# A recurrent layer's block inverse packed into half the columns, and its key and output blocks run with wide matmuls

## The chip, the cores and the metric

The kernel runs on one core of a Trainium2 chip. The metric is the time of one execution on the device, in microseconds (us). TensorE does the matmuls, VectorE (DVE) and ScalarE (ACT) the elementwise work, GpSimd (POOL) small copies; SyncE (SP) issues the DMAs. Each engine works through its instructions in a fixed order.

## What is computed

The reference is a trunk of two layers over 256 tokens with 2048 channels: a differential attention with a gated convolution MLP, then a gated DeltaNet layer with another such MLP. The change is in the DeltaNet layer. Cut to that layer:

```python
qkv = silu(causal_dwconv(qkv, conv_w))          # of h @ w_in
q, k = l2_norm(q), l2_norm(k)                   # 16 heads, repeated to 32
low = where(strict, (k_beta @ k.T) * decay, 0)  # per head and chunk of 64 tokens
a_mat = low + eye(64)                           # unit lower triangular
u = triangular_solve(a_mat, v_beta)
w = triangular_solve(a_mat, k_beta * exp(g_c))
# then a scan over the chunks with state, q, k, u, w
o = rms_norm(o, norm_g) * silu(z)
x = x + o @ w_out
```

## The kernel before

**Two-part matmuls.** Every weight tile comes from DRAM in 512 KB pieces (`raw`, L86), called tiles below. ScalarE casts a piece to a short float type (`whi`, L89), and VectorE subtracts to get the rest (`wlo`, L90). Four buffers of each kind rotate. Activations are held in two parts as well, 256 columns each. The function `dense` multiplies such a piece: 4 row blocks by 2 column tiles. *Wide* means one matmul of `whi` with both activation parts (512 columns, L151) and one of `wlo` with the first part (256 columns, L152), into two halves of a PSUM bank that are added afterwards. *Narrow* means three matmuls of 256 columns (L151, L152, L154) into one half, so there is nothing to add.

**The DeltaNet stage** (`gdn`) goes through 4 batches of 4 key heads. Per batch it runs 4 key blocks (`k`), a value block (`v`), two gate blocks (`z`, in `dense_tok`), 3 more value blocks, and then the 8 output blocks of the batch before. A key or value block is 16 row blocks long, so 4 tiles of 8 steps; an output block has 8 row blocks and 2 tiles. A small gate projection of 4 tiles runs ahead of the first batch. Key blocks and the last batch's value blocks are narrow, the other value blocks wide; an output block is narrow in batches 0 to 2 for its first four column blocks.

Beside this stream, coroutines do the rest, and each advances when `dense` calls `tick()` after a tile: `keys` (squares, sums, exponentials of the decay rows `lt` that come back from DRAM through `grow`, products, copies of the diagonal blocks into `cc` by GpSimd), `invert` (the inverse of all 32x32 diagonal blocks of a batch), `levels` (joins the 32s to 64s and 128s), `group` (solves and output). A scheduler then sets each engine's order by its own timeline.

**The inverse.** Each of the four groups of 32 partitions holds 16 blocks of 32x32 per batch. `cc` has 32 columns, of which 16 are filled; VectorE transposes it so that partition = block, and 16 of every 32 partitions work on zeros. A loop over 30 columns j then multiplies and subtracts on `Ti` (L667, L670), with `(31-j) * j` elements each time. Two transposes give `ttc` and `tcc`. The tiles share the tag `s4` with three buffers.

**The edges of the stage.** The constants `con` (identity and mask) are loaded at its start, into memory that the layer before used until its end.

Of the kernel before, what the change touches and what calls it, by code (L numbers as in the profile page):

```python
# [16 lines left out]
P = 128  # L17
T = 256
D = 2048
KD = D // P  # L20
# [6 lines left out]
class Trunk:  # L27
# [514 lines left out]
    def gdn(self, w_gate, w_in, w_z, w_out, nb, hb, gate_ap, const_ap, conv_col, ng, done):  # L542
# [7 lines left out]
        nc, tc, mp = self.nc, self.tc, self.mp  # L550
        nq = nb * hb
# [3 lines left out]
        with tc.tile_pool(name="gd", bufs=1) as gd:  # L555
# [3 lines left out]
            ident, mask = con[:, :P], con[:, P:]  # L559
# [9 lines left out]
                nc.gpsimd.memset(Tas[i][:64], 0.0)  # L569
            quad = [slice(32 * s, 32 * s + 32) for s in range(4)]  # L570
            flat = "p i c -> p (i c)"
            gates, lows = {}, []

            def lin(w, wide):
# [19 lines left out]
            def keys(hq, c, cc, b0, res):  # L594

                sq = gd.tile([P, 2, T], F32, tag="qs", name="qs", bufs=2)
                nc.scalar.square(sq, c)
                sp = gd.tile([P, 2, 2, T], F32R, tag="qp", name="qp", bufs=1)
                lows.append(self.split(sp, sq))

                def fetch():
                    d = gd.tile([P, 2, 384], F32, tag="lt", name="lt", bufs=hb)
                    nc.sync.dma_start(d, gates["rows"][2 * hq:2 * hq + 2, :].unsqueeze(0).to_broadcast([P, 2, 384]))
                    return d

                d = fetch() if "rows" in gates else None
                yield
                yield
                while "rows" not in gates:
                    yield  # L610
                if d is None:
                    d = fetch()
                    yield
                    yield
                    yield
                gc = gates["col"]
                dv = d[:, :, :T].rearrange("p v (t c) -> p v t c", t=2)
                m4 = mask.unsqueeze(1).unsqueeze(1).to_broadcast([P, 2, 2, P])
                pn = mp()
                sums = self.total(pn, [sp])  # L620
                while len(lows) < 2:
                    yield
                with tc.issue_after(lows[max(hq, 1)].ins):
                    nc.vector.tensor_tensor(dv, dv, m4, ALU.add)
                with self.lnexp(sums):
                    self.rsqrt(sq, self.apart(pn), 1)
                    for v in range(2):
                        for t, s in ((1, d[:, v, :P]), (0, d[:, v, P:])):
                            nc.scalar.activation(s, s, AF.Exp, bias=gc[:, t, 2 * hq + v:2 * hq + v + 1])
                nc.vector.tensor_tensor(c, c, sq, ALU.mult)  # L630
                q, k = c[:, 0, :], c[:, 1, :]
                yield
                yield
                prods = []
                for r in (k, q):
                    p = mp()
                    nc.tensor.matmul(p[:, :P], k[:, P:], r[:, P:], start=True, stop=True)
                    nc.tensor.matmul(p[:, P:384], k[:, :P], r, start=True, stop=True)  # L638
                    prods.append(p)
                lt = d  # L640
                qkt = gd.tile([P, 2, 384], F32, tag="qkt", name="qkt", bufs=hb)
                for v in range(2):
                    nc.vector.scalar_tensor_tensor(
                        qkt[:, v], prods[1][:, :384], P ** -0.5, d[:, v], ALU.mult, ALU.mult)
                    nc.vector.tensor_tensor(lt[:, v], prods[0][:, :384], d[:, v], ALU.mult)
                for v in range(2):
                    b = b0 + v
                    lv = lt[:, v, :T].rearrange("p (t c) -> p t c", t=2)
                    for r in quad:
                        nc.gpsimd.tensor_copy(  # L650
                            cc[r, :, 2 * b:2 * b + 2].rearrange("p c t -> p t c"), lv[r, :, r])
                    res.append((lt[:, v], qkt[:, v]))

            def invert(cc, lqs, inv):

                while len(lqs) < 2 * hb:
                    yield
                x = gd.tile([P, 32, 32], F32, tag="s4", name="X", bufs=3)
                nc.vector.transpose(x.rearrange(flat), cc.rearrange(flat))
                t = gd.tile([P, 32, 32], F32, tag="s4", name="Ti", bufs=3)  # L660
                nc.vector.tensor_scalar(t, x, -1.0, None, ALU.mult)
                nc.vector.memset(t.rearrange(flat)[:, ::33], 1.0)
                for j in range(1, 31):
                    m = 31 - j
                    tmp = gd.tile([P, T], F32, tag="tmp", name="tmp", bufs=1)
                    w = tmp[:, :m * j].rearrange("p (i c) -> p i c", c=j)
                    nc.vector.tensor_tensor(  # L667
                        w, x[:, j + 1:, j:j + 1].to_broadcast([P, m, j]),
                        t[:, j:j + 1, :j].to_broadcast([P, m, j]), ALU.mult)
                    nc.vector.tensor_tensor(t[:, j + 1:, :j], t[:, j + 1:, :j], w, ALU.subtract)  # L670
                    if j % 3:
                        yield
                ttc = gd.tile([P, 32, 32], F32, tag="s4", name="ttc", bufs=3)
                nc.vector.transpose(ttc.rearrange("p m i -> p i m"), t)
                tcc = gd.tile([P, 32, 32], F32, tag="s4", name="tcc", bufs=3)
                nc.vector.transpose(tcc.rearrange("p m c -> p c m"), t.rearrange("p i c -> p c i"))
                inv += [ttc, tcc]

            def levels(lqs, inv, gs, done):
# [137 lines left out]

            def out(b, acts):
                for blk in range(KD // 2):
                    wide = b == nb - 1 or blk >= KD // 4  # L820
                    ps = self.dense(w_out[b * (KD // 2) + blk], 2 * hb, lambda k: self.await_(acts, k), wide=wide)
                    self.add_out(blk, ps, done if b == nb - 1 else None, wide)

# [2 lines left out]
            pend = None  # L826
            for b in range(nb):
                heads = range(b * hb, (b + 1) * hb)
                cc = gd.tile([P, 32, 32], F32, tag="s4", name="Cc", bufs=3)
                nc.gpsimd.memset(cc, 0.0)  # L830
                lqs, inv, solved, acts, zts = [], [], [], [], {}
                groups = [range(i, i + gh) for i in range(0, hb, gh)]
                plan = [("k", i) for i in range(hb)] + [("v", 0)] + [("z", g) for g in range(len(groups))]
                for op, i in plan + [("v", i) for i in range(1, hb)]:
                    if op == "k":
                        hq = heads[i]
                        c = convs(lin(w_in[hq * 2], False), (hq, nq + hq))
                        self.spawn(keys(hq, c, cc, 2 * i, lqs))
                        if i == hb - 1:
                            self.spawn(invert(cc, lqs, inv))  # L840
                            self.spawn(levels(lqs, inv, range(len(groups)), solved))
                    elif op == "z":
                        gr = groups[i]
                        zt = zts[i] = gd.tile([P, 2, gv, P], F32, tag="vz", name="zt", bufs=4)
                        ps = self.dense_tok(w_z[heads[gr[0]] // 2], KD, self.h_acts)
                        for t in range(2):
                            nc.scalar.activation(zt[:, t].rearrange(flat), ps[:, t, :], AF.Silu,  # L847
                                                 scale=self.rstdc[:, t:t + 1])
                    else:
                        gi = i // gh  # L850
                        gr = groups[gi]
                        if i == gr[0]:
# [223 lines left out]
```

## Time and profile before

| | |
|---|---|
| median of 3 runs | 2532.01 us (2531.71 to 2532.07) |
| the profiled execution | 2531.32 us, span 2529.5 us |
| instructions | 42709 |
| granted TensorE clock | 1.00 throughout |
| DMA | 487.25 MB, mean 193 GB/s |
| DeltaNet stage | from 1053.9 us (first matmul of its gate block) to 1848.9 us |

Times in rows are us from the span's start. A row of the order of time has start, duration, engine, line, operation, tiles written and read, matrix size, shape and count; in brackets stands how long the engine was idle before, and what ended that. A row of a group ends with count, busy time, mean ns of one, idle time before. Matmuls overlap in the records: what one costs in a stream is the distance between starts, not its duration.

### The profile page before, as it was taken

Reading aid. Unit: us, or ns where it says so; the run is one execution under the profiler, and the core shown is the slowest. Engines: PE = TensorE matmul, PEld = TensorE weight load, DVE = VectorE, ACT = ScalarE, POOL = GpSimd, SP = SyncE. Lnnn points to the kernel's source line nnn. Section 1 sums busy time; section 2 is a strip of 40 time slices with the busy share of each in tenths; the row PEclk is TensorE's granted clock in tenths of the full one; section 3 lists DMA queues with packets and bytes.
Section 4 is the critical chain, followed back from the end, with each engine's and each line's share of the span. In section 5 each row is a group of like instructions: output and inputs, shape, how many; then the busy total and the mean of one; then the engine's idle time right before and its main releaser. Section 6 shows DMA issues by size and latency. Waiting matters only on the chain.

```text
span 2529.5 us, 42709 instructions
## 1 busy us (share of the span) xinstructions
PE 2522.4 (100%) x16727; PEld 2330.5 (92%) x16727; DVE 1913.4 (76%) x2822; ACT 1501.8 (59%) x2082; POOL 97.2 (4%) x189
## 2 busy tenths in 40 slices
PE   9999999999999999999999999999999999999999
PEld 8998899999999999999989989999999999999998
DVE  8886677777777555689879789788787777776544
ACT  7766656666666444485674675674566666665343
POOL 0000000000000000011110021021000000000000
PEclk9999999999999999999999999999999999999999
DMA  7555566666666666666555555555466666666665
GB/s 257 175 183 175 167 204 201 201 201 201 201 201 202 201 199 201 203 189 207 163 170 197 162 183 190 163 186 174 162 201 200 202 201 201 201 202 205 210 207 157
DMA packets 138203, 487.25 MB, mean 193 GB/s; under 512 B 15473, under 2 KB 18449, under 8 KB 138001
## 3 DMA queue, kind: packets, MB, share of 16 engines
q1 hardware_dynamic: 137712, 484.17, 60.0%
q8 instruction: 131, 2.15, 0.4%
q14 instruction: 72, 0.58, 0.1%
q10 hardware_dynamic: 288, 0.35, 0.0%
HBM read 482.32 MB, written 2.15 MB: 192 GB/s over the span
## 4 chain that ended last, share of the span: by engine, by line
PE 99%; DMA 1%; DVE 0%; ACT 0%; SPq 0%; issue 0%; ACTq 0%
PE ps L151 50%; PE ps L152 27%; PE ps L154 4%; PE ps L221 3%; PE ps L220 3%; PE ps L222 3%; PE mp L765 2%; PE mp L151 1%; PE mp L329 1%; PE mp L638 1%; PE mp L152 0%; PE ps L123 0%; PE mp L730 0%; PE mp L748 0%; PE mp L810 0%; PE mp L466 0%
## 5 line engine op out<-in xcount | busy, mean ns | idle before, releaser
L90 DVE TENSOR_TENSOR wlo<-raw,whi 128x1024 fp32r<-128x1024 f32 (+2 forms) x911 | 1102.6, 1212 | 510.2 <-ACT whi L89 502.0
L89 ACT CAST whi<-raw 128x1024 fp32r<-128x1024 f32 (+2 forms) x911 | 944.1, 1038 | 849.9 <-PE ps L151 627.1
L151 PE MATMUL ps<-h,whi 128*128 128x512 f32 (+1 forms) x4208 | 1348.0, 366 | 0.0
L152 PE MATMUL ps<-h,wlo 128*128 128x256 f32 x4208 | 1151.2, 274 | 0.6 <-DVE wlo L90 0.6
L151 PEld LDWEIGHTS ps<-h,whi 128*128 128x128 f32 x4208 | 797.2, 189 | 93.6 <-ACT zt L847 0.2
L152 PEld LDWEIGHTS ps<-h,wlo 128*128 128x128 f32 x4208 | 807.7, 192 | 2.0 <-DVE wlo L90 0.9
L151 PE MATMUL ps<-ac,whi 128*128 128x512 f32 x1546 | 506.8, 382 | 0.0
L152 PE MATMUL ps<-ac,wlo 128*128 128x256 f32 x1546 | 421.2, 273 | 0.0
L151 PEld LDWEIGHTS ps<-ac,whi 128*128 128x128 f32 x1546 | 292.1, 189 | 40.6 <-PE ps L151 0.2
L152 PEld LDWEIGHTS ps<-ac,wlo 128*128 128x128 f32 x1546 | 296.8, 192 | 0.1
L154 PE MATMUL ps<-h,whi 128*128 128x256 f32 x656 | 181.8, 277 | 0.0
L151 PE MATMUL ps<-oc,whi 128*128 128x512 f32 (+1 forms) x512 | 159.7, 344 | 0.0
L220 PE MATMUL ps<-whi,h 128*128 128x512 f32 x384 | 146.4, 381 | 0.0
L221 PE MATMUL ps<-wlo,h 128*128 128x512 f32 x384 | 145.8, 380 | 0.0
L222 PE MATMUL ps<-whi,h 128*128 128x512 f32 x384 | 145.8, 380 | 0.0
L310 DVE SCALAR_TENSOR_TENSOR cv<-u,fcols,cv 128x255 f32<-128x255 f32 (+1 forms) x344 | 142.9, 477 | 0.0
L152 PE MATMUL ps<-oc,wlo 128*128 128x256 f32 x512 | 140.7, 275 | 0.0
L154 PEld LDWEIGHTS ps<-h,whi 128*128 128x128 f32 x656 | 125.8, 192 | 0.2
L151 PEld LDWEIGHTS ps<-oc,whi 128*128 128x128 f32 x512 | 97.4, 190 | 8.0
L152 PEld LDWEIGHTS ps<-oc,wlo 128*128 128x128 f32 x512 | 98.3, 192 | 0.3
L308 ACT ACTIVATE cv<-u,fcols 128x256 f32<-128x256 f32 x172 | 93.9, 593 | 0.6 <-DVE u L205 0.5
L310 DVE SCALAR_TENSOR_TENSOR cv<-u,cols,cv 128x255 f32<-128x255 f32 (+2 forms) x192 | 84.2, 478 | 0.4 <-ACT cv L306 0.3
(222 smaller groups left out, 2178.7 us busy)
## 6 DMA issues: line engine op xcount, KB each, us to landing
raw<-w_up SPq DMA_DIRECT2D x344, 512.0 KB, 4.7
raw<-w_down SPq DMA_DIRECT2D x160, 512.0 KB, 3.7
raw<-w_in SPq DMA_DIRECT2D x128, 512.0 KB, 4.6
raw<-w_z SPq DMA_DIRECT2D x64, 512.0 KB, 3.8
raw<-w_out SPq DMA_DIRECT2D x64, 512.0 KB, 4.3
raw<-w_qk SPq DMA_DIRECT2D x56, 512.0 KB, 4.6
raw<-w_v SPq DMA_DIRECT2D x32, 512.0 KB, 3.5
raw<-w_o SPq DMA_DIRECT2D x32, 512.0 KB, 4.7
```

Source lines behind the costliest of these rows:

```text
L89: self.cast = nc.scalar.copy(hi[:, :, s], raw[:, :, s])
L90: nc.vector.tensor_tensor(lo[:, :, s], raw[:, :, s], hi[:, :, s].bitcast(F32), ALU.subtract)
L151: nc.tensor.matmul(bank[c][:, :n], hi[:, k, s], self.turns(a[:, :n // T, :]), start=first, stop=False)
L152: nc.tensor.matmul(bank[c][:, :T], lo[:, k, s], self.turns(a[:, :1, :]), start=False, stop=last and wide)
L154: nc.tensor.matmul(bank[c][:, :T], hi[:, k, s], self.turns(a[:, 1:, :]), start=False, stop=last)
L220: nc.tensor.matmul(ps[:, c, :], ah, wh, start=first, stop=False)
L221: nc.tensor.matmul(ps[:, c, :], ah, wl, start=False, stop=False)
L222: nc.tensor.matmul(ps[:, c, :], al, wh, start=False, stop=last)
L308: nc.scalar.activation(out, u, AF.Identity, bias=bias, scale=taps[n - 1])
L310: nc.vector.scalar_tensor_tensor(out[:, j:], u[:, :T - j], taps[n - 1 - j], out[:, j:], ALU.mult, ALU.add)
L329: last = self.nc.tensor.matmul(out, self.onesr, self.pairs(p[:, j]), start=i + j == 0, stop=i + j == n)
L765: nc.tensor.matmul(p[:, v, :], l(v), r[:, v, :], start=i == 0, stop=i == len(terms) - 1)
```

## The change

The inverse uses all 32 partitions of a group: `cc` has only the 16 filled columns, the transpose reads it twice (16 partitions each), and `Ti` holds the even columns of the inverse in one set of 16 partitions and the odd ones in the other, 16 columns wide. The loop has 31 steps with `(31-j) * (j//2 + 1)` elements. `Ti` is filled by GpSimd with zeros and with ones where the diagonal lies; which parity a partition has comes from `half`, which VectorE reduces once from `ident` (a part of `con`). `tcc` comes from `Ti`, and `ttc` from `tcc`. Each tile has a tag and one buffer of its own. `keys` yields three times instead of two. Key blocks of batches 0 to 2 and all output blocks are wide.

```diff
+            nl = 4 * hb
+            half = gd.tile([P, 2], F32, tag="half", name="half")
...
-                yield
-                yield
+                for _ in range(3):
+                    yield
...
-            def invert(cc, lqs, inv):
+            def invert(b, cc, lqs, inv):
+                while not lqs:
+                    yield
+                if b == 0:
+                    nc.vector.tensor_reduce(half, ident.rearrange("p (q a c) -> p a q c", q=4, a=2), AX.XY, ALU.add)
+                t = gd.tile([P, 32, 16], F32, tag="Ti", name="Ti")
+                nc.gpsimd.memset(t, 0.0)
+                for a in range(2):
+                    nc.gpsimd.tensor_copy(t.rearrange(flat)[:, 16 * a::33], half[:, a:a + 1].to_broadcast([P, 16]))
                 while len(lqs) < 2 * hb:
                     yield
-                x = gd.tile([P, 32, 32], F32, tag="s4", name="X", bufs=3)
-                nc.vector.transpose(x.rearrange(flat), cc.rearrange(flat))
-                t = gd.tile([P, 32, 32], F32, tag="s4", name="Ti", bufs=3)
-                nc.vector.tensor_scalar(t, x, -1.0, None, ALU.mult)
-                nc.vector.memset(t.rearrange(flat)[:, ::33], 1.0)
-                for j in range(1, 31):
-                    m = 31 - j
+                x = gd.tile([P, 32, 32], F32, tag="X", name="X")
+                nc.vector.transpose(x, cc.unsqueeze(2).to_broadcast([P, 32, 2, nl]))
+                for j in range(31):
+                    m, n = 31 - j, j // 2 + 1
...
-                    w = tmp[:, :m * j].rearrange("p (i c) -> p i c", c=j)
+                    w = tmp[:, :m * n].rearrange("p (i c) -> p i c", c=n)
...
-                    nc.vector.tensor_tensor(t[:, j + 1:, :j], t[:, j + 1:, :j], w, ALU.subtract)
+                    nc.vector.tensor_tensor(t[:, j + 1:, :n], t[:, j + 1:, :n], w, ALU.subtract)
...
-                nc.vector.transpose(ttc.rearrange("p m i -> p i m"), t)
-                nc.vector.transpose(tcc.rearrange("p m c -> p c m"), t.rearrange("p i c -> p c i"))
+                tcc = gd.tile([P, nl, 32], F32, tag="tcc", name="tcc")
+                nc.vector.transpose(tcc.rearrange("p m (c a) -> p c a m", a=2), t.rearrange("p i c -> p c i"))
+                ttc = gd.tile([P, nl, 32], F32, tag="ttc", name="ttc")
+                nc.vector.transpose(ttc.rearrange(flat), tcc.rearrange(flat))
...
-                    wide = b == nb - 1 or blk >= KD // 4
+                    wide = True
...
-                cc = gd.tile([P, 32, 32], F32, tag="s4", name="Cc", bufs=3)
-                nc.gpsimd.memset(cc, 0.0)
+                cc = gd.tile([P, 32, nl], F32, tag="Cc", name="Cc")
...
-                        c = convs(lin(w_in[hq * 2], False), (hq, nq + hq))
+                        c = convs(lin(w_in[hq * 2], b<nb-1), (hq, nq + hq))
```

In the new file later lines have moved: L629 became L631, L591 L593, L597 L599, L704 L711, the key block's narrow eviction L196 became a copy L582, an addition L583 and a scaling L205.

The scheduler's order moves with it. VectorE at the start of the stage, before (L343 adds the last block of the layer before into x; the 512-wide L90 is the gate block's last piece, the 1024-wide the first key block's):

```order
L90 TENSOR_TENSOR wlo<-raw,whi 128x512
L343 TENSOR_TENSOR x<-ps,x 128x512
L90 TENSOR_TENSOR wlo<-raw,whi 128x1024
L235 SCALAR_TENSOR_TENSOR h<-x,cols,h 128x256 x2
L247 TENSOR_TENSOR ss<-ss,sq 128x256
```

The same place now:

```order
L90 TENSOR_TENSOR wlo<-raw,whi 128x512
L343 TENSOR_TENSOR x<-ps,x 128x512
L661 TENSOR_REDUCE half<-con 128x2
L90 TENSOR_TENSOR wlo<-raw,whi 128x1024
L235 SCALAR_TENSOR_TENSOR h<-x,cols,h 128x256 x2
L247 TENSOR_TENSOR ss<-ss,sq 128x256
```

The reduction of `half` from `con` is put ahead of the first key block's piece.

ScalarE in batch 0, around the first exponentials of the decay rows (L629), before:

```order
L89 CAST whi<-raw 128x1024
L321 CAST qp<-qs 128x512
L591 ACT_TABLE_LOAD
L591 ACTIVATE cv<-cv 128x512
L89 CAST whi<-raw 128x1024
L597 ACTIVATE qs<-cv 128x512
L629 ACT_TABLE_LOAD
L629 ACTIVATE lt<-lt,gc 128x128
```

And now (L631):

```order
L89 CAST whi<-raw 128x1024
L321 CAST qp<-qs 128x512
L89 CAST whi<-raw 128x1024
L593 ACT_TABLE_LOAD
L593 ACTIVATE cv<-cv 128x512
L599 ACTIVATE qs<-cv 128x512
L89 CAST whi<-raw 128x1024
L582 COPY u<-ps 128x512
L631 ACT_TABLE_LOAD
L631 ACTIVATE lt<-lt,gc 128x128
```

Two casts stand between L321 and the exponentials instead of one, and the new copy L582 too.

TensorE where the joining of batch 0's inverse begins (L704, reading `tcc`), before, in the second key block of batch 1:

```order
L151 MATMUL ps<-h,whi 128x256
L704 MATMUL mp<-tcc,lt 32x32 x32
L748 MATMUL mp<-con,cv 128x128 x4
L152 MATMUL ps<-h,wlo 128x256
L154 MATMUL ps<-h,whi 128x256
```

And now (L711), in the last value block of batch 0:

```order
L151 MATMUL ps<-h,whi 128x512
L711 MATMUL mp<-tcc,lt 32x32 x32
L152 MATMUL ps<-h,wlo 128x256
L151 MATMUL ps<-h,whi 128x512
L152 MATMUL ps<-h,wlo 128x256
```

It has moved six tiles ahead in the stream of blocks.

More of the change, by code (lines that the diff above doesn't have):

```diff
@@ L665, in invert @@
+                nc.vector.transpose(x, cc.unsqueeze(2).to_broadcast([P, 32, 2, nl]))
+                for j in range(31):
+                    m, n = 31 - j, j // 2 + 1
                     tmp = gd.tile([P, T], F32, tag="tmp", name="tmp", bufs=1)
-                    w = tmp[:, :m * j].rearrange("p (i c) -> p i c", c=j)
+                    w = tmp[:, :m * n].rearrange("p (i c) -> p i c", c=n)
                     nc.vector.tensor_tensor(
-                        w, x[:, j + 1:, j:j + 1].to_broadcast([P, m, j]),
-                        t[:, j:j + 1, :j].to_broadcast([P, m, j]), ALU.mult)
@@ L670, in invert @@
-                    nc.vector.tensor_tensor(t[:, j + 1:, :j], t[:, j + 1:, :j], w, ALU.subtract)
+                        w, x[:, j + 1:, j:j + 1].to_broadcast([P, m, n]),
+                        t[:, j:j + 1, :n].to_broadcast([P, m, n]), ALU.mult)
+                    nc.vector.tensor_tensor(t[:, j + 1:, :n], t[:, j + 1:, :n], w, ALU.subtract)
                     if j % 3:
                         yield
-                ttc = gd.tile([P, 32, 32], F32, tag="s4", name="ttc", bufs=3)
-                nc.vector.transpose(ttc.rearrange("p m i -> p i m"), t)
@@ L675, in invert @@
-                tcc = gd.tile([P, 32, 32], F32, tag="s4", name="tcc", bufs=3)
-                nc.vector.transpose(tcc.rearrange("p m c -> p c m"), t.rearrange("p i c -> p c i"))
+                tcc = gd.tile([P, nl, 32], F32, tag="tcc", name="tcc")
+                nc.vector.transpose(tcc.rearrange("p m (c a) -> p c a m", a=2), t.rearrange("p i c -> p c i"))
+                ttc = gd.tile([P, nl, 32], F32, tag="ttc", name="ttc")
+                nc.vector.transpose(ttc.rearrange(flat), tcc.rearrange(flat))
@@ L836, in gdn @@
                         hq = heads[i]
-                        c = convs(lin(w_in[hq * 2], False), (hq, nq + hq))
+                        c = convs(lin(w_in[hq * 2], b<nb-1), (hq, nq + hq))
                         self.spawn(keys(hq, c, cc, 2 * i, lqs))
                         if i == hb - 1:
-                            self.spawn(invert(cc, lqs, inv))
+                            self.spawn(invert(b, cc, lqs, inv))
                             self.spawn(levels(lqs, inv, range(len(groups)), solved))
```

## The prediction

> **What bounds the kernel now.** I read the page's first parts, then who TensorE waited for, then stretches of the DeltaNet stage (1054 to 1849 us), where the change lies. First the page's busy times and, below them, the chain that ended last by engine:
>
> ```profile
> PE 2522.4 (100%) x16727; PEld 2330.5 (92%) x16727; DVE 1913.4 (76%) x2822; ACT 1501.8 (59%) x2082; POOL 97.2 (4%) x189
> PE 99%; DMA 1%; DVE 0%; ACT 0%; SPq 0%; issue 0%; ACTq 0%
> ```
>
> A busy TensorE can still be one that stutters, so the waits decide. This is the only wait of TensorE that the list of waits has after the first layer's start (0.6 us in total, once):
>
> ```profile
> PE ps L152 <- DVE wlo L90: 0.6, 1, 0.6
> ```
>
> So the kernel is TensorE's stream of matmuls. Time is won only by a shorter stream, and lost only where VectorE (DVE) or ScalarE (ACT) hands over a weight tile too late. Four stretches of the stage; the columns are TensorE, weight loads, VectorE, ScalarE and GpSimd busy, each with its count, then granted clock, DMA share and GB/s:
>
> ```profile
> 1053.90:1107.00 53.10, 53.10 (x466) 52.65 (x465) 44.10 (x80) 38.25 (x55) 3.92 (x6) 1.00 0.70 224
> 1165.00:1196.40 31.40, 31.40 (x193) 28.88 (x192) 30.75 (x59) 17.68 (x22) 0.00 (x0) 1.00 0.62 200
> 1350.40:1371.80 21.40, 21.40 (x194) 21.40 (x193) 21.26 (x39) 10.95 (x13) 0.00 (x0) 1.00 0.63 210
> 1394.50:1456.30 61.80, 61.80 (x668) 60.98 (x667) 43.51 (x74) 38.87 (x60) 1.69 (x3) 1.00 0.49 159
> ```
>
> The first and last are narrow key blocks (the first with the gate block ahead), the second wide value blocks beside the inverse, the third narrow output blocks beside the inverse. Beside the inverse VectorE is at 98 and 99%; in the key stretches at 83 and 70%. Weight loads fill 100% of the narrow output stretch and 92% of the wide one. The clock is 1.00 throughout.
>
> **The change part by part.**
>
> *Narrow blocks made wide.* A narrow block issues three 256-column matmuls per weight tile, a wide one a 512-column and a 256-column matmul: the same 768 columns, one weight load less. The changed blocks hold 12 x 16 x 2 = 384 key triples and 12 x 8 x 2 = 192 output triples, 576 in all. What a triple and a pair take is read from starts in the order of time. The 64 triples of the third stretch, from the first row to the last (the next block's first):
>
> ```profile
> 1350.36 0.28 PE L151 MATMUL ps<-oc,whi 128*128 128x256 f32 x1
> 1350.47 0.28 PE L152 MATMUL ps<-oc,wlo 128*128 128x256 f32 x1
> 1350.59 0.28 PE L154 MATMUL ps<-oc,whi 128*128 128x256 f32 x1
> ...
> 1371.80 0.38 PE L151 MATMUL ps<-oc,whi 128*128 128x512 f32 x1
> L154 PE MATMUL ps<-oc,whi 128*128 128x256 f32 x64 | 17.6, 275 | 0.0
> ```
>
> (1371.80 - 1350.36) / 64 = 0.3350 us. The 96 pairs of the second stretch:
>
> ```profile
> 1165.02 0.38 PE L151 MATMUL ps<-h,whi 128*128 128x512 f32 x1
> ...
> 1196.46 0.28 PE L151 MATMUL ps<-h,whi 128*128 128x256 f32 x1
> L151 PE MATMUL ps<-h,whi 128*128 128x512 f32 x96 | 31.5, 382 | 0.0
> ```
>
> (1196.46 - 1165.02) / 96 = 0.3275 us. A triple becomes a pair for 7.5 ns less: 576 x 7.5 = **4.3 us off TensorE's stream**. Reading error is 0.01 us at either end, so under 0.2 us in the sum. The Trainium skill, page "TensorE: Matmul & The Clock Gate", section "Back-to-back issue gap", gives an isolated gap of N / 2.4 + 2.5 ns: 327.5 ns for the triple and 325.0 for the pair, thus 1.4 us in the sum by it. The rows are of this very stream, so 4.3 is used.
>
> *What the wide form adds beside the stream.* A narrow key block leaves PSUM by one VectorE operation (the first row), a wide one by a ScalarE copy, an addition and a scaling; a wide output block adds into x twice instead of once:
>
> ```profile
> L196 DVE TENSOR_TENSOR u<-ps,rstd 128x512 f32<-128x512 f32 x20 | 13.7, 686 | 2.2 <-PE ps L154 2.1
> L580 ACT COPY u<-ps 128x512 f32<-128x512 f32 x12 | 6.9, 576 | 0.0
> L581 DVE TENSOR_TENSOR u<-ps,u 128x512 f32<-128x512 f32 x12 | 8.2, 682 | 0.0
> L205 DVE TENSOR_TENSOR u<-u,rstd 128x512 f32<-128x512 f32 x98 | 67.7, 691 | 2.9
> L343 DVE TENSOR_TENSOR x<-ps,x 128x512 f32<-128x512 f32 x98 | 67.3, 687 | 10.3 <-PE ps L152 6.9 <-PE ps L154 2.1
> ```
>
> Per key block 0.69 us on VectorE and 0.58 on ScalarE, per output block 0.69 on VectorE: 16.5 us of VectorE and 6.9 of ScalarE in all.
>
> *The inverse.* One batch's, between 1149 and 1212 us:
>
> ```profile
> L667 DVE TENSOR_TENSOR tmp<-X,Ti 128x30 f32<-128x30 f32 (+14 forms) x30 | 9.8, 327 | 0.6
> L670 DVE TENSOR_TENSOR Ti<-Ti,tmp 128x30 f32<-128x30 f32 (+14 forms) x30 | 9.8, 327 | 0.4
> L676 DVE STREAM_TRANSPOSE tcc<-Ti 128x1024 f32<-128x1024 f32 x1 | 2.1, 2095 | 0.0
> L674 DVE STREAM_TRANSPOSE ttc<-Ti 128x1024 f32<-128x1024 f32 x1 | 2.0, 2004 | 0.0
> L659 DVE STREAM_TRANSPOSE X<-Cc 128x1024 f32<-128x1024 f32 x1 | 1.2, 1248 | 0.9 <-POOL Cc L650 0.9
> L667 DVE TENSOR_TENSOR tmp<-X,Ti 128x30 f32<-128x30 f32 x2 | 0.4, 178 | 0.0
> L667 DVE TENSOR_TENSOR tmp<-X,Ti 128x240 f32<-128x240 f32 x2 | 0.8, 406 | 0.0
> ```
>
> Before: 19.6 + 4.1 + 1.2 = 24.9 us, and the fill of Ti beside it. The last two rows give 145 ns for an operation and 1.09 ns an element. The new loop has 62 operations and 2 x 2856 elements: 9.0 + 6.2 = 15.2 us. Its last two transposes have half the elements (2.1), the first as many, read or written another way (1.2 to 2.1). That is 18.5 to 19.4 us: some 5.5 to 6.4 us less per batch, 22 to 26 over four. On VectorE it pays for the 16.5 us above; on the path it is **worth 0**, since no inverse held TensorE up. The fill of Ti and its ones move to GpSimd, which idles 96%.
>
> *A new wait at the stage's start.* In the order, the reduction that makes half stands on VectorE ahead of the first key block's L90. It reads con, whose DMA is issued only when the layer before has ended:
>
> ```profile
> 1054.13 0.33 SPq L558 DMA_DIRECT2D con<-const  x1
> con<-const SPq DMA_DIRECT2D x1, 128.0 KB, 4.7
> 1055.35 0.68 DVE L343 TENSOR_TENSOR x<-ps,x 128x512 f32<-128x512 f32 x1
> 1056.56 1.23 DVE L90 TENSOR_TENSOR wlo<-raw,whi 128x1024 fp32r<-128x1024 f32 x1 [0.53 <-ACT whi L89]
> 1058.85 0.39 PE L152 MATMUL ps<-h,wlo 128*128 128x256 f32 x2
> L471 DVE TENSOR_REDUCE nm<-sc 128x1 f32<-128x128 f32 x16 | 4.5, 280 | 0.2
> ```
>
> con lands at 1054.13 + 4.7 = 1058.8; the reduction, priced by the last row, ends at 1059.1; L90, L235 and L247 are queued behind it, and L90 ends at 1060.3. TensorE wants that tile with the second of the two matmuls at 1058.85, about 1058.96: **1.4 us lost**. Bounds: 0 (con lands 1.4 us sooner) and 2.0. L235 and the second L90 then end by 1062.6, and TensorE, itself later, comes for them at 1063.
>
> *The one wait that goes.* In batch 0 the exponentials (L629) waited for the decay rows from DRAM, and casts stood behind them:
>
> ```profile
> 1103.84 0.69 DVE L624 TENSOR_TENSOR lt<-lt,con 128x512 f32<-128x512 f32 x1 [1.93 <-DMA lt<-grow]
> 1105.28 1.50 ACT L629 ACTIVATE lt<-lt,gc 128x128 f32<-128x128 f32 x4
> 1110.57 1.05 ACT L89 CAST whi<-raw 128x1024 fp32r<-128x1024 f32 x1
> 1111.96 1.21 DVE L90 TENSOR_TENSOR wlo<-raw,whi 128x1024 fp32r<-128x1024 f32 x1
> 1113.22 0.38 PE L152 MATMUL ps<-h,wlo 128*128 128x256 f32 x1 [0.57 <-DVE wlo L90]
> ```
>
> In the new order one more cast stands between the key's L321 and those exponentials, and the keys start one tile later, so the tiles behind are ready one to two tiles of 8 pairs (2.6 to 5.2 us) sooner against the wait: **0.7 us gained** (the pair's start came 0.95 us after L151 instead of 0.22). DMA issue of grow moves behind one more weight load on SP; that load's buffer is free by about 1095, when grow's rows are written, so I cost it at nothing; without that cover, one tile, 2.6 us, is what the decay rows would be late. What is late next in the key stretches is a tile such as this one, ready at 1278.27 for a TensorE that asks at 1279.31:
>
> ```profile
> 1277.05 1.22 DVE L90 TENSOR_TENSOR wlo<-raw,whi 128x1024 fp32r<-128x1024 f32 x1
> 1279.31 0.38 PE L221 MATMUL ps<-wlo,h 128*128 128x512 f32 x1
> ```
>
> Its margin is 1.0 us. There the solve of batch 0 and the keys of batch 1 fell together on ScalarE and VectorE. In the new order the solve begins in the last value block instead of the second key block, six tiles sooner, and so is out of the way sooner; the key stretches above have 17 to 30% of VectorE free. I take nothing for it, with bounds 0 and the rival below.
>
> **Sum:** -4.3 + 1.4 - 0.7 = -3.6 us. The profiled execution took 2531.32 us (span 2529.5 and 1.8 around it), so 2527.7; it lies 0.7 under the median of the runs, 2532.01, which gives **2528.4**. A measurement of this kernel can tell about 0.2% from no change, 5.1 us: under 2526.9 is faster, over 2537.1 slower.
>
> **The rivals.**
> - *No new wait* (0.28): con lands early enough, or TensorE makes the 1.4 us up. -4.3 - 0.7 = -5.0, so 2527.0, on the edge of faster. For it: landing is a median of one DMA. Against: it is issued at a fixed event, and the order puts the reduction first.
> - *Key stretches run late on VectorE and ScalarE* (0.17), the case on the other side. Every key block adds 0.69 + 0.58 us to a chain that hands over between the two engines; it decides once the margin (1.0 us at 1279) is used up in each batch. Fully exposed: 12 x 1.27 = 15.2, so 2532.01 - 4.3 + 1.4 - 0.7 + 15.2 = 2543.6. With half of it 2536.0. For it: that margin of 1.0 us came about although VectorE was not full, so the waits between the two engines count, not their sums. Against: the free VectorE share, the solve's earlier place, and one more tile of delay (three yields for two). I give the half 0.09 and the full price 0.08.
> - *The third weight load is hidden after all* (0.05), and triple and pair are equal in the key blocks: 0 + 1.4 - 0.7, so 2532.7. Against: in the narrow key stretch the loads are as full (52.65 of 53.10 us) as in the output stretch that was measured. The skill's formula above goes halfway there, to 2531.3.
>
> **How the numbers follow.** The forecast has 0.47, the rivals 0.50, and 0.03 is left for what I don't see. The range 2526.3 to 2536.0 takes in the forecast with its bounds (1.4 as 0 to 2.0), the first and third rival and the second up to half its price; out stay the full price and what lies beyond either end. Faster: half of the first rival and a little of the forecast, 0.18. Slower: the full price and some of the half, 0.12. Same: 0.70.
>
> **What would show it.** L154 on h falls from 656 to 272 calls and on oc from 192 to none; a changed block's pairs start 0.3275 us apart. L661 starts at about 1058.8 of the old time, and TensorE's list of waits has one of over 1 us on L90 there. The wait at 1113 is gone. I am wrong if TensorE has new waits on L90 in batches 0 to 2 (the second rival), or if the changed blocks' pairs are not 7 ns shorter than the triples (the third).

## The result and the profile after

| | before | after |
|---|---|---|
| median | 2531.98 us (16 runs, 2531.42 to 2534.40) | 2536.27 us (16 runs, 2534.94 to 2538.27) |
| span of the profiled execution | 2529.5 us | 2535.1 us |

The ratio is 1.0017, with a 95% interval of 1.0011 to 1.0024: 4.3 us slower. The forecast was 2528.4 with a range up to 2536.0: it had the wrong sign, and the time lies 0.3 us above the range. The change, 0.17%, is within the 0.2% that the prediction counted as no change. The clock is 1.00 in both, and the time outside the DeltaNet stage is alike (1734.5 us of the span before, 1734.7 after).

The page after, with busy times and the chain that ended last:

```profile
PE 2522.6 (100%) x16151; PEld 2311.7 (91%) x16151; DVE 1908.0 (75%) x2847; ACT 1507.9 (59%) x2094; POOL 99.5 (4%) x197
PE 95%; ACT 3%; DVE 1%; DMA 1%; issue 1%; SPq 0%; ACTq 0%; DVEq 0%
```

The 576 matmuls are gone (16727 to 16151), VectorE has 5.4 us less to do, and TensorE is as busy as before. The chain was 99% TensorE; now 4% runs over ScalarE and VectorE. The DeltaNet stage as one stretch, before and then after (TensorE, weight loads, VectorE, ScalarE and GpSimd busy, then clock, DMA share, GB/s):

```profile
1053.90:1848.90 795.00, 794.41 (x6311) 747.55 (x6310) 669.13 (x1112) 504.46 (x699) 97.02 (x185) 1.00 0.56 181
```

```profile
1053.90:1854.30 800.40, 794.43 (x5735) 728.97 (x5734) 663.34 (x1137) 510.11 (x711) 99.32 (x193) 1.00 0.57 179
```

TensorE's idle time is the length less the busy time: 0.6 us before, 6.0 after. That is the whole 5.4 us. The busy time has not fallen with the stream, since the longer joins and the matmuls drawn out ahead of a wait (both below) count as busy. The list of waits says where it stands (us in total, times, longest); the rows of the first layer's start are left out:

```profile
PE ps L221 <- DVE wlo L90: 1.8, 2, 1.1
PE mp L884 <- DVE glin L196: 1.4, 1, 1.4
...
PE ps L152 <- DVE wlo L90: 1.1, 1, 1.1
PE mp L329 <- ACT qp L321: 1.1, 2, 0.6
...
PE ps L220 <- ACT whi L89: 0.4, 1, 0.4
```

A wait shows here a little short: the matmul ahead of it is drawn out in the records, so that the distance between starts exceeds a matmul's own by 0.15 to 0.3 us more than the idle time (the first below by 1.30 us, for 1.13 idle). By such excess of the starts, in order of time: 1.3 us at 1060, 1.6 at 1073, 3.2 in batch 0's first gate block (1119 to 1135), and 0.65 and 0.76 at 1469 and 1662. The first two, in order of time:

```profile
1058.87 0.29 DVE L661 TENSOR_REDUCE half<-con 128x2 f32<-128x128 f32 x1 [2.86 <-DMA con<-const]
1059.07 1.22 DVE L90 TENSOR_TENSOR wlo<-raw,whi 128x1024 fp32r<-128x1024 f32 x1
1060.34 0.38 PE L152 MATMUL ps<-h,wlo 128*128 128x256 f32 x1 [1.13 <-DVE wlo L90]
...
1068.92 1.23 DVE L90 TENSOR_TENSOR wlo<-raw,whi 128x1024 fp32r<-128x1024 f32 x1 [1.86 <-ACT whi L89]
1070.06 0.42 DVE L289 TENSOR_TENSOR ms<-ms,rstd 128x258 f32<-128x258 f32 x1
...
1073.14 0.42 DVE L196 TENSOR_TENSOR glin<-ps,rstd 128x256 f32<-128x256 f32 x1
...
1073.62 0.34 PE L884 MATMUL mp<-con,glin 64*128 64x64 f32 x2 [1.43 <-DVE glin L196]
```

The forecast wait for con is there to the tenth. Behind it an L90 stands ahead of the norm's last steps (L289 to L292) and itself waits for its cast, so `glin` is late for the gate's transpose, which had no wait before. Then batch 0's first gate block:

```profile
1098.88 0.34 SPq L922 DMA_DIRECT2D grow<-early  x1
1104.31 1.76 SPq L605 DMA_DIRECT2D lt<-grow  x4
1104.37 0.63 ACT L599 ACTIVATE qs<-cv 128x512 f32<-128x512 f32 x1 [1.78 <-DMA grow<-early]
...
1116.67 1.48 ACT L631 ACTIVATE lt<-lt,gc 128x128 f32<-128x128 f32 x4
1118.05 0.61 ACT L321 CAST qp<-qs 128x512 fp32r<-128x512 f32 x1
1118.56 1.05 ACT L89 CAST whi<-raw 128x1024 fp32r<-128x1024 f32 x1
...
1119.95 1.21 DVE L90 TENSOR_TENSOR wlo<-raw,whi 128x1024 fp32r<-128x1024 f32 x1
1121.21 0.48 PE L221 MATMUL ps<-wlo,h 128*128 128x512 f32 x1 [1.07 <-DVE wlo L90]
```

The second pair of exponentials, which before ended by 1110.2, now ends at 1118.2, and the cast behind it comes too late. One thing is no wait, and no list shows it. In the join of the 32-blocks, the order of time has TensorE's 64 `px` and 32 `py` matmuls of a batch, before (L716, L718) and then after (L723, L725):

```profile
1215.25 0.22 PE L716 MATMUL mp<-ttc,pc 32*32 32x32 f32 x2
1215.26 0.21 PE L718 MATMUL mp<-pc,TT 32*32 32x32 f32 x1
...
1216.38 0.38 PE L154 MATMUL ps<-h,whi 128*128 128x256 f32 x1
```

```profile
1204.97 0.22 PE L723 MATMUL mp<-ttc,pc 32*32 32x32 f32 x2
1204.98 0.21 PE L725 MATMUL mp<-pc,TT 32*32 32x32 f32 x1
...
1205.50 0.67 PE L723 MATMUL mp<-ttc,pc 32*32 32x32 f32 x32
1206.10 0.38 PE L152 MATMUL ps<-h,wlo 128*128 128x256 f32 x1
...
1206.95 0.69 PE L725 MATMUL mp<-pc,TT 32*32 32x32 f32 x16
1207.57 0.38 PE L152 MATMUL ps<-h,wlo 128*128 128x256 f32 x1
```

Before, 96 of them alternated px, px, py and took 1.13 us. Now the second head group has its 32 px first (0.60 us from 1205.50) and its 16 py in a row later (0.62 us). In the program px uses two 32x32 corners of the array and py a third; the time of one matmul, 12 ns in turn on three corners, 19 ns on two and 39 ns on one, goes with the number of corners. The batch's join takes 1.13 + 0.62 us. That is so in batches 0 to 2, so the stage's joins take 6.4 us instead of 4.7: 1.7 us.

### The profile page after: what moved, and what is told of

Read it like the earlier page. It is cut to its first block, busy times and chain, and to the rows that moved or that the text cites. A ratio compares the mean times of both kernels' runs of the same rounds, so it can differ in the third digit from the quotient of the medians.

```text
span 2535.1 us, 41611 instructions
## 1 busy us (share of the span) xinstructions
PE 2522.6 (100%) x16151; PEld 2311.7 (91%) x16151; DVE 1908.0 (75%) x2847; ACT 1507.9 (59%) x2094; POOL 99.5 (4%) x197
## 4 chain that ended last, share of the span: by engine, by line
PE 95%; ACT 3%; DVE 1%; DMA 1%; issue 1%; SPq 0%; ACTq 0%; DVEq 0%
PE ps L151 51%; PE ps L152 26%; PE ps L221 3%; PE ps L222 3%; PE ps L220 3%; PE mp L772 2%; PE mp L151 1%; PE ps L154 1%; ACT whi L89 1%; PE mp L329 1%; PE mp L152 0%; DVE wlo L90 0%; ACT L593 0%; PE ps L123 0%; ACT lt L631 0%
## 5 line engine op out<-in xcount | busy, mean ns | idle before, releaser
L90 DVE TENSOR_TENSOR wlo<-raw,whi 128x1024 fp32r<-128x1024 f32 (+2 forms) x911 | 1104.6, 1214 | 514.4 <-ACT whi L89 506.8
L151 PE MATMUL ps<-h,whi 128*128 128x512 f32 (+1 forms) x4208 | 1369.5, 376 | 0.0
L151 PEld LDWEIGHTS ps<-h,whi 128*128 128x128 f32 x4208 | 796.1, 189 | 102.9
L151 PE MATMUL ps<-oc,whi 128*128 128x512 f32 x512 | 171.2, 384 | 0.0
L221 PE MATMUL ps<-wlo,h 128*128 128x512 f32 x384 | 145.9, 380 | 1.8 <-DVE wlo L90 1.8
L343 DVE TENSOR_TENSOR x<-ps,x 128x512 f32<-128x512 f32 x110 | 75.8, 689 | 13.9 <-PE ps L152 12.5
L221 PEld LDWEIGHTS ps<-wlo,h 128*128 128x128 f32 x384 | 72.6, 189 | 12.2 <-DVE wlo L90 2.4
```

Of the source, the lines that this page charges most:

```text
L90: nc.vector.tensor_tensor(lo[:, :, s], raw[:, :, s], hi[:, :, s].bitcast(F32), ALU.subtract)
L151: nc.tensor.matmul(bank[c][:, :n], hi[:, k, s], self.turns(a[:, :n // T, :]), start=first, stop=False)
L221: nc.tensor.matmul(ps[:, c, :], ah, wl, start=False, stop=False)
L343: self.nc.vector.tensor_tensor(x, part, x, ALU.add)
```

## The experiments

Theory 1: the loss is the wait for con and what it makes late. Theory 2: it is the wide key blocks, which put ScalarE and VectorE behind in batch 0. Theory 3: it is the new order of the joins. (The first expectations add switches between fp32 and fp32r matmuls to theory 3; no run takes those apart.) Times are medians of 11 executions, 4 in run 3; ratios are against the kernel before on the same chip (2531.8 to 2531.9 us). The difference of two runs is uncertain by 0.5 to 0.9 us, and by more where runs 3, 7, 8 and 15 take part, whose executions scatter over 3 to 7 us. "By the starts" means the excess described above.

**1. The wait for con taken away.** The planner is told to issue the reduction only after the first key split:

```diff
+                    with tc.issue_after(lows[0].ins):
-                    nc.vector.tensor_reduce(half, ...)
+                        nc.vector.tensor_reduce(half, ...)
```

> The changed kernel with one edit: the reduction of con into half is held back until the first key split (L322) has been issued, so VectorE no longer stands at con's landing at the start of the DeltaNet stage. Theory 1 (the wait for con sets off a chain: 1.3 us at 1060 us, 1.4 us at the transposes of glin, and gate rows some 3 us late, from which come the waits of 3.2 us in total in batch 0's first z block): all of these go, about -5 us, so 2531 us, 1.0 us below before; TensorE waits over 250 ns before 1200 us fall from about 6 us to under 1.5 us. Theory 2 (the wide key blocks with their ScalarE copy and three pauses put VectorE behind in batch 0's z block): only the first two waits go, -2.7 us, 2533.5 us, and the waits near 1119 and 1133 us stay. Theory 3 (the regrouped joins and the switches between fp32 and fp32r matmuls carry the loss): under -1.5 us.

2535.0 us, ratio 1.0013 (1.0004 to 1.0022): only 1.3 us less than the changed kernel. TensorE's waits of this run:

```profile
PE ps L221 <- DVE wlo L90: 2.4, 3, 1.0
...
PE mp L329 <- ACT qp L321: 1.1, 2, 0.6
PE mp L885 <- DVE glin L196: 0.9, 1, 0.9
```

The wait at 1060 us is gone. Those for `glin` and in the gate block are 0.5 us shorter each, by the starts, but stay, although grow's rows come 2.8 us sooner (L599, which stands behind them, at 1101.6) and TensorE only 1.8. A new wait of 1.1 us, the third of the first row, came at 1290, in batch 1, so the 1.3 us are not simply con's. Theory 1 as a whole falls.

**2. The reduction added to the kernel before,** where the changed kernel has it.

> The kernel before with only the reduction of con into half added at the place where the changed kernel has it; its result is used by nothing. Theory 1: the start of the DeltaNet stage loses the 1.3 us at 1060 us and the 1.4 us at the transposes of glin, and the gate rows come some 3 us later; 2534.7 us or, with waits in batch 0's z block as well, up to 2537 us. Theory 2: only the two waits, 2534.7 us, and none over 0.5 us in batch 0's z block. Theory 3: the wait for con is made up later, 2532 to 2533 us.

2533.0 us, ratio 1.0004 (0.9995 to 1.0013), so about 1.0 us and not clear of noise; of the expectations only the last case, 2532 to 2533 us, holds. In its trace the first wait is 0.8 us by the starts, and there is no wait for `glin` and none in the gate block: con's wait alone brings neither.

**3. Only the wide blocks,** with the old inverse and two pauses.

> The kernel before with only the wide blocks (keys of the first three batches and all output blocks); the inverse and the two pauses of keys as before. Theory 1: the stream saves 4.2 us and nothing at the start is lost: 2528 to 2529 us. Theory 2: the waits of batch 0's first z block come with the wide keys, so the saving is mostly eaten: 2530.5 to 2532 us. Theory 3: switches are saved by this part as well, joins as before: 2528 us.

2552.9 us, ratio 1.0083 (1.0069 to 1.0096): far outside every expectation. ScalarE and then TensorE in batch 1, two rows of TensorE's list, and a stretch in batch 2 with columns as for the stage above:

```profile
1320.53 1.28 ACT L847 ACT_TABLE_LOAD   x1
1321.83 2.42 ACT L847 ACTIVATE zt<-ps,rstd 128x512 f32<-128x512 f32 x4
1323.14 0.48 PE L151 MATMUL ps<-h,whi 128*128 128x512 f32 x1 [3.24 <-ACT zt L847]
PE ps L151 <- ACT zt L847: 6.5, 2, 3.2
PE ps L221 <- DVE wlo L90: 1.6, 2, 0.8
...
1519.00:1524.00 5.00, 3.50 (x12) 2.79 (x12) 3.11 (x6) 1.02 (x2) 0.00 (x0) 0.66 0.59 191
```

The planner has put the silu reads of both gate blocks together (x4, in batches 1 and 2; before it was x2 and x2), so the PSUM bank of the first is not free when the next value block wants it. That is 6.8 of the stage's 18.8 us more, by the starts. The rest is a wait of 3.6 us at 1520 on the keys of batch 2 (L637), some 4 us of waits in the last solve (1807 to 1818), 2.4 on its output `oc`, and batch 0's. The clock adds to it: after the waits that end at 1520 and 1527 it is 0.66 and 0.57 in the stretches (1.00 elsewhere), and the distances between starts are nearly double for some 3 us each, so about 3 us in all, as an estimate. The L221 row has batch 0's waits again, here without `half`, so they come with the wide keys: a point for theory 2.

**4. Only the new inverse.**

> The kernel before with only the new inverse (with its reduction of con); key and output blocks narrow and two pauses as before. Theory 1: the losses at the start without the saving: 2534.7 to 2537 us. Theory 2: the two waits at the start alone: 2534.7 us. Theory 3 (the copies of the inverse and the joins after it stand elsewhere): 2536 us or more, with matmuls of the joins dearer by 1.5 us in total and no more than 1.3 us lost before 1070 us.

2535.0 us, ratio 1.0012 (1.0003 to 1.0021). That is the time of theories 1 and 2, but not by their waits: there is none for `glin` and none in the gate block. The waits are 0.9 us at 1060 and 1.3 at 1115 (0.7 before); px and py together take 6.6 us in the stage, before 4.7. A point for the mechanism of theory 3, whose time (2536 or more) was too high.

**5. The joins put back in turn,** on top of run 1:

```diff
+                for g in gs:
+                    nc.gpsimd.tensor_copy(TTs[g][quad[1], :, quad[1]], ttc[quad[1], nm * g:nm * g + nm, :])
...
-                    for s in (1, 3, 0, 2):
+                    for s in (3, 0, 2):
```

> As the run with half held back (2535.0 us), with one more edit: the GpSimd copies of ttc into the second diagonal block of TT are issued first for both head groups, so that the program order of TensorE again has px, px, py in turn in every join (in the changed kernel 16 px and then 8 py stand together in half of the joins). Theory 3 (regrouped joins cost time because px and py no longer overlap): the 384 matmuls of 32 columns of these two lines take 4.6 us again rather than 6.4, and the kernel falls by 1.5 to 2 us, to 2533.2 us. Theory 2 (wide keys of batch 0): the joins' change is hidden or made up elsewhere, 2535 us.

2533.2 us, ratio 1.0005 (0.9996 to 1.0014): 1.8 us less than run 1, with px and py in turn and 1.14 to 1.22 us a batch. Theory 3 holds for its 1.8 us.

**6. Batch 0's keys narrow,** on top of run 1:

```diff
-                        c = convs(lin(w_in[hq * 2], b<nb-1), (hq, nq + hq))
+                        c = convs(lin(w_in[hq * 2], 0 < b < nb - 1), (hq, nq + hq))
```

> As the run with half held back (2535.0 us), with the four key blocks of batch 0 narrow again and those of batches 1 and 2 wide. Theory 2 (the wide keys of batch 0 bring the wait at glin, 1.1 us, and those at 1118 and 1132 us in the first z block, 2.5 us): both go, 128 matmul triples give back 1.0 us of the saving, so -2.5 us: 2532.5 us. Theory 1 or 3: the waits stay and the lost saving comes on top, 2536 us.

2533.5 us, ratio 1.0007 (0.9999 to 1.0016): 1.5 us less, where theory 2 gave 2.5. The waits for `glin` and on L90 are gone, as it had it; two new ones came in batch 1. The joins, 5.9 us for run 1's 6.4, have 0.5 of the gain. New waits, and ScalarE at the first exponentials of the decay rows, run 6 and then run 1:

```profile
PE mp L639 <- DVE cv L632: 1.4, 1, 1.4
...
PE mp L329 <- ACT whi L89: 0.5, 1, 0.5
...
1104.53 1.28 ACT L631 ACT_TABLE_LOAD   x1 [0.36 <-DMA lt<-grow]
1105.82 1.49 ACT L631 ACTIVATE lt<-lt,gc 128x128 f32<-128x128 f32 x4
```

```profile
1109.88 1.50 ACT L631 ACTIVATE lt<-lt,gc 128x128 f32<-128x128 f32 x4
```

With narrow keys the exponentials wait for the rows from DRAM. With wide keys the rows land 0.7 us later (1105.1), but the exponentials, 4.1 us later, don't wait for them: ScalarE is busy without a break from 1101.6 (L599) to the exponentials, with two more casts and a silu with its table load (L593) ahead of them.

**7. Only the output blocks wide,** in the kernel before.

> The kernel before with only the output blocks wide; keys, inverse and pauses as before. By 192 triples of 7.5 ns the stream saves 1.4 us: 2530.5 us if nothing else moves. If wide blocks delay what stands beside them whatever their kind (theory 2 for all blocks), it is 2532 us or more.

2534.8 us, ratio 1.0014 (1.0005 to 1.0023): 2.9 us slower where 1.4 were to be gained. The list of waits, and the end of the last batch in order of time:

```profile
PE ps L151 <- DVE oc L814: 2.3, 1, 2.3
PE ps L151 <- DVE x L343: 1.8, 2, 1.4
...
1814.78 1.40 DVE L814 SCALAR_TENSOR_TENSOR oc<-mp,cols,oc 128x512 fp32r<-128x512 f32 x2
1815.58 0.48 PE L151 MATMUL ps<-oc,whi 128*128 128x512 f32 x1 [2.28 <-DVE oc L814]
```

In the last batch the stream runs out before the solve's output is there. The shorter stream alone doesn't explain it: the last two L814 start at 1814.78 and 1815.44, before at 1807.91 and 1810.30, so the solve itself comes 5 to 7 us later in the new order, and the stream is only 1.4 shorter.

**8. Run 3 with three pauses.**

> The run with only the wide blocks (2552.9 us, 21 us above before, with waits of 3.2 us each for the silu reads of the z blocks) with the three pauses of the changed kernel instead of two. If the pause is what keeps the keys' exponentials clear of the z blocks, most of the 21 us goes: 2530 to 2534 us. If it is the shorter inverse that the wide keys need, it stays above 2545 us.

2535.8 us, ratio 1.0018 (1.0009 to 1.0027), above the 2530 to 2534 expected. The silu reads are x2 and x2 again. So the third pause takes away 17 of run 3's 21 us; what is left has the wait for `oc` (2.3 us) and one for x (2.2), as in run 7, and batch 0's (1.7 on L221).

**9 to 12. Mended kernels.** All four have `half` held back and the joins in turn. Run 9 has batch 0's keys narrow and three pauses only in wide key blocks; run 10 the same with two pauses everywhere; run 11 narrow keys throughout, two pauses; run 12 as run 11 with the output blocks as before.

```diff
-                for _ in range(3):
+                for _ in range(2 + (0 < hq // hb < nb - 1)):
```

```diff
-                for _ in range(3):
+                for _ in range(2):
```

The first edit is run 9's, the second that of the other three.

> The changed kernel with half held back, the copies spread (as in the run of 2533.2 us), batch 0's keys narrow, and three pauses only in the wide key blocks (batches 1 and 2), two in the narrow ones. If the parts add: 2533.5 us (batch 0 narrow) less 1.8 us (spread joins) less 0.7 us (the wait for qp at 1661 us, in batch 3's narrow keys, which the kernels with two pauses don't have): 2531.0 us, 0.9 us below before. If the waits only move on (to the first wide keys of batch 1, 2.2 us at 1269 us in the run before, and more): 2532 to 2534 us.

> As the run just before, with two pauses everywhere. If two pauses put the exponentials of wide key blocks into the z blocks whatever the inverse (21 us in the run of wide blocks alone), it loses 5 us or more in batches 1 and 2: above 2536 us. If that came of the longer inverse, the waits for qp go in batch 2 too: 2530 to 2531 us.

> The kernel before with the new inverse, half held back, copies spread, and all output blocks wide; all key blocks narrow with two pauses. If the shorter inverse is what the wide output blocks of the last batches need (they lost 2.3 us at oc and 1.4 us at x with the old one): the stream's 1.4 us are kept, 2530.5 us, and neither wait is in the trace. If not: 2533 us or more, with both waits.

> The kernel before with the new inverse alone, half held back and copies spread. If the 3.1 us that the new inverse cost alone (2535.0 us) are the wait for con (1.3 us) and the regrouped joins (1.8 us) and nothing else, it equals before: 2531.9 us, within 0.5. If the inverse costs by other shifts too, 2533 us or more.

| run | us | ratio (95%) |
|---|---|---|
| 12, new inverse | 2530.0 | 0.9993 (0.9984 to 1.0002) |
| 11, and wide output blocks | 2528.5 | 0.9987 (0.9978 to 0.9996) |
| 10, and wide keys in batches 1 and 2 | 2527.2 | 0.9982 (0.9973 to 0.9991) |
| 9, and three pauses in those | 2528.6 | 0.9988 (0.9979 to 0.9997) |

From 12 to 11 the output blocks bring 1.6 us (costed: 1.4), from 11 to 10 the keys 1.2 (costed: 256 x 7.5 ns = 1.9), each uncertain by 0.7 to 0.8; from 10 to 9 the third pause costs 1.4. All four came out 1.9 to 2.8 us under their expectations, and run 12's 1.9 is in each of them: the wait of 0.7 us at 1113 is gone too, and L329 takes 7.5 us of the stage, not 8.1. Run 10 beats both kernels. Its stage and all its waits after the first layer:

```profile
1053.90:1845.10 791.20, 790.98 (x5864) 731.47 (x5863) 661.29 (x1134) 511.00 (x710) 99.31 (x193) 1.00 0.56 182
PE mp L329 <- ACT qp L321: 0.2, 1, 0.2
```

TensorE idles 0.2 us of 791.

**13. All keys wide, two pauses** (run 5 with two pauses; run 10 with batch 0 wide).

> The changed kernel with half held back and copies spread (2533.2 us), with two pauses instead of three; beside the run of 2527.2 us it has batch 0's key blocks wide. If the wide blocks of batch 0 bring the waits of its first z block (2.9 us) and at glin (0.6 us), whatever the pauses: 2527.2 + 3.5 - 1.0 (the saved triples) = 2529.7 us, with waits near 1118 and 1132 us. If the third pause brings them: 2526.3 us, without these waits.

2529.4 us, ratio 0.9992 (0.9983 to 1.0001), as the case of wide blocks gave (2529.7). Waits:

```profile
PE ps L221 <- DVE wlo L90: 1.6, 2, 0.9
...
PE mp L887 <- DVE glin L196: 0.5, 1, 0.5
...
PE ps L220 <- ACT whi L89: 0.4, 1, 0.4
```

Batch 0's wide keys thus cost 2.2 us net, 3.2 before their 1.0 of saving, and these are the waits that run 10 lacks. Beside run 5, the third pause taken out gains 3.8 us: its waits at 1290, 1468 and 1660, 2.6 us by the starts, are gone.

**14. Run 10 with the reduction back at con's landing.**

> The run of 2527.2 us with the reduction of con back at its old place, so that VectorE stands at con's landing. If con's wait costs no more than TensorE shows at 1060 us (0.8 to 1.3 us) as long as batch 0's keys are narrow: 2528.0 to 2528.5 us. If the late gate rows bring waits in batch 0's z block by themselves (theory 1): 2530 us or more.

2531.1 us, ratio 0.9997 (0.9988 to 1.0006): 3.9 us more than run 10, where the wait alone was expected. By the time that is the case of theory 1, but not by the place. Two of its waits in order of time:

```profile
1060.24 0.38 PE L152 MATMUL ps<-h,wlo 128*128 128x256 f32 x1 [0.91 <-DVE wlo L90]
...
1291.73 0.48 PE L221 MATMUL ps<-wlo,h 128*128 128x512 f32 x1 [1.03 <-DVE wlo L90]
```

The second, in batch 1's gate block, 230 us later, can't come of the same delay: the one edit has changed the planner's order on ScalarE from batch 0 on. In run 10 three casts (1281.75 to 1285.7) stand ahead of batch 1's exponentials there, in run 14 the exponentials stand between two casts (1284.8 and 1289.1). By the starts its waits are 1.1 us at 1060, 0.6 at 1114 (the one of the kernel before is back), and 0.4 and 1.2 in batch 1's gate block, 3.3 in all. Batch 0's gate block has none, though the decay rows land at 1105.0, as late as in runs 1 and 13 (1105.1): rows as late as these bring none by themselves.

**15. The changed kernel with two pauses** and nothing else.

> The changed kernel with two pauses instead of three and nothing else. If the third pause brings the two waits for qp (1469 and 1661 us) and batch 0's waits stay: 2536.3 - 1.4 = 2534.9 us. If it brings batch 0's waits too: 2531.5 us. If two pauses clash with the z blocks as in the run of wide blocks with the old inverse: 2540 us or more.

2537.0 us, ratio 1.0022 (1.0013 to 1.0031): 0.7 more, which its scatter (2535.3 to 2540.9) does not tell from nothing, and not the 1.4 less. The two waits for `qp` are gone, but a wait of 2.5 us came at 1280 us (batch 1); the first two waits of the stage are 0.7 us longer together, and those in batch 0's gate block as much shorter. In the mended kernel the same edit gains 3.8 us (run 5 to run 13): a pause has no price of its own here.

## Why the prediction was wrong

**Right.** The stream: triples without a wait among them take 335.0 ns from start to start before (mean of 764 in the stage), pairs 327.5 ns after (1175), so 576 x 7.5 ns = 4.3 us less, as costed. The formula of the Trainium skill (page "TensorE: Matmul & The Clock Gate", section "Back-to-back issue gap") would have given 1.4; the measurement decides for the rows, and run 12 to run 11 (1.6 us for 192 triples) too. The inverse: 31.5 + 31.6 + 5.0 + 4.5 + 2.8 = 75.4 us for four, 18.9 each (18.5 to 19.4 forecast). The wait at con: 1.3 us (1.4).

**Wrong.** The step that failed is the one that took the feeders of the key blocks and the joins at nothing, and the third pause as relief. That the time came within 0.3 us of the half price of the second rival (2536.0) is chance: the half stood for 7.6 us spread over twelve blocks.

- *"Key stretches run late on VectorE and ScalarE"*, a rival at 0.17, was what happened, but in batch 0 alone: 3.2 us by runs 13 and 10, of 4 x 1.27 = 5.1. I had averaged it over twelve blocks; batches 1 and 2 kept most of their saving. In every trace with wide keys in batch 0 (after, runs 1, 3, 5, 8, 13, 15) the first exponentials start at 1109.8 or later and its first gate block has 2.4 to 3.4 us of waits by the starts, most of them on L90, the prediction's own sign of this rival; in every one with narrow keys (before and the other runs) they start at 1107.2 or sooner, and it has at most 0.2. Run 6 beside run 1 shows that it is ScalarE's queue that makes them late, not the rows from DRAM.
- *"The one wait that goes", -0.7 us:* the wait at 1113 went, but its cause, casts queued behind exponentials, came back in the gate block, where the term stopped looking. The decay rows are used 4.4 us later (L626 at 1108.24, L624 at 1103.84), of which 2.9 are the two waits ahead of them; that grow was taken "at nothing" is not what failed, since the waits are there with earlier rows too (runs 1 and 13) and not in run 14, with rows as late as in those two.
- *The joins* were no term at all. The prediction read `tcc` and `ttc` only as transposes of a known price. The new kernel's order of GpSimd's copies changed that of the joins on TensorE: 1.8 us (run 5).
- *"One more tile of delay (three yields for two)"* was counted as relief. With the old inverse it is (run 3 to run 8, 17 us). With the new one it costs 3.8 us (run 13 to run 5) and 1.4 (run 10 to run 9); in the changed kernel it brings the two waits for `qp`, 1.4 us, but nothing clear in the total (run 15).
- *"L235 and the second L90 then end by 1062.6, and TensorE, itself later, comes for them at 1063"* was true, and followed the queue too short a way. The norm's chain to `glin` is queued behind: up to 1.6 us. By run 2 (none) and run 3 (0.6 us without `half`) it takes the wide first key block to be seen.
- *The inverse "worth 0 on the path"* held only for the stream as it was. With wide output blocks the old inverse has a wait for `oc` and one for x (run 7: 2534.8), the new one neither (run 11: 2528.5). Whether its length does that or the order that comes with it, these two runs don't tell.

Sum, by the starts in the changed kernel: -4.3 (stream) + 1.3 (con) + 1.6 (`glin`) + 3.2 - 0.7 (gate block, less the wait at 1113) + 1.7 (joins) = +2.8, and the two waits for `qp`, 1.4, make +4.2 of the stage's +5.4; the remaining 1.2 us is spread (the transposes that were L810 have 0.5 of it). Still open is why the planner writes these orders: that one edit (a reduction, a pause) moves waits 200 us away is shown by runs 14 and 15, but not by which of its rules.

## What to carry over

When TensorE is full, a shorter stream pays only where every feeder has slack at that place: price a rival batch by batch (here the loss was in the first). In a kernel whose order a planner writes, an edit is its own price plus a new order, so read the changed order on every engine, also for matmuls that stood in turn and now stand in a row. And take a change of several parts apart before dropping it: the parts here gained 4.5 us once the reduction, the copies, the pauses and batch 0 were put right, while the inverse or the wide output blocks alone, unmended, each lost 3.

## What the runs showed of the hardware

32x32 matmuls on different corners of the array overlap: 96 of px, px, py on three corners took 1.13 us, 12 ns each, 32 of px on two corners 0.60 us, 19 ns each, and 16 of py on one corner 0.62 us, 39 ns each. The Trainium skill says that tiles can work in parallel (page "TensorEngine Tiling (Array Packing)", section "Key Properties"), and the rows agree; what it gives as an issue floor, about 25 ns (page "TensorE: Matmul & The Clock Gate", section "Back-to-back issue gap"), lies between the last two.

The granted clock fell in run 3's trace alone: after a wait of TensorE of 3.4 us (to 1520.0), and again after one of 3.2 us (to 1526.7), matmuls started about twice as far apart for some 3 us (512 columns: 427 ns for 218). After another wait of 3.2 us in the same trace (to 1323.1) they did not.
